# Expert weights loaded as half the rows by 512 columns, and units of work of four output tiles

## The chip, the cores and the metric

One NeuronCore of a Trainium2 chip runs the whole program. The metric is device time in microseconds (us) of one execution. Engines are named as the profile names them: PE (TensorE matmuls), PEld (TensorE weight loads), DVE (VectorE), ACT (ScalarE), POOL (GpSimd), SP (SyncE, which only issues DMAs here).

## The reference

A decoder layer on 1024 tokens of width 1024. A mixer (gated linear attention and a diagonal state-space model) comes first; the change does not touch it. The second half is a mixture of 32 experts, of which each token takes four:

```python
def expert_block(args):
    xblk, e = args
    gu = xblk @ w_gu[e] + b_gu[e]              # w_gu[e]: 1024 x 2048
    g, up = gu[:, :D_FF], gu[:, D_FF:]
    g = jnp.minimum(g, SWIGLU_LIMIT)
    up = jnp.clip(up, -SWIGLU_LIMIT, SWIGLU_LIMIT)
    act = (up + 1.0) * (g * jax.nn.sigmoid(SWIGLU_ALPHA * g))
    return act @ w_down[e] + b_down[e]         # w_down[e]: 1024 x 1024
...
out = jnp.zeros((N + 1, D_), f32).at[tok_buf].add(yb.astype(f32) * w_buf[:, None])[:N]
```

All weights are float32, 12 MB an expert. After the experts come a norm and the residual.

## The kernel before

**Sizes.** Experts are sorted by the number of their tokens; the expert of rank r has room for `CAPS[r]` tokens (396 for the first, 36 for the last). I call this number C. Eight groups of four ranks (`GROUPS`) are worked on one after the other: [204, 96, 172, 108], [184, 116, 180, 104], [272, 92, 140, 80], [164, 128, 164, 120], [396, 40, 88, 56], [260, 60, 148, 112], [248, 48, 192, 92], [252, 68, 228, 36] tokens, in this order within a group.

**Weights.** A piece of weights (`chunks`) is 1 MB: all 1024 rows by 256 columns, which lie in SBUF as [128 partitions, 8 row blocks, 256 columns]. SP loads it into one of six staging slots (`ST`, the A buffers 0 to 5). `split_chunk` (L1594 to L1597) makes two fp16 parts of it: ACT writes the high part (`wh`, L1596), then DVE the low part (`wl`, L1597), side by side in one of seven slots (`WH`, `WL`, in the buffers B0, B1, C0, C1, E0, E1, A6, used in turn). After a piece is split, SP may load the piece six further on into its staging slot.

**Products.** `products` (L1615 to L1620) makes one output tile, 128 columns of weights by C tokens: for each of eight row blocks three matmuls (high by high, high by low, low by high), 24 in all, into PSUM.

**Units.** The work on PE is a list of units. In a group's gate-up stage there are four rounds (c = 0 to 3), and in each round one unit for each of the four experts: two tiles of the gate from one piece, then two tiles of the up part from the next piece, 96 matmuls. In the down stage each expert has four units in a row, each of two tiles from one piece, 48 matmuls. Where C is over 256 a unit is halved (one tile of each kind), since two tiles don't fit one PSUM bank; both halves then use the same pieces.

**Order.** The program is written out in one loop over the units, each engine runs its own instructions in the order written. For unit i the loop writes: what is left of the unit two before (`second`: the activations as fp16 parts), the evictions of the unit before (`first`: ACT reads PSUM at L1661, L1664 or L1683; DVE clips and multiplies), the splits, and then the products of unit i. The splits go as far as this line allows (L1760), where `done` is the last piece that the units before the last one are through with and `NWS` is 7:

```python
split_to((max(done + NWS, need) if i > 2 else need) + 1)
rest = run_unit(*u)
```

In the down stage the loop also writes, behind a unit's products, the transposes and fp16 parts of the next group's tokens (`xg_split`, L1610), and for finished halves of an expert's results `put_out`/`moe_out`: PE transposes (L1697), ACT copies into one of three buffers (L159, tile A), POOL scatters with accumulation to `ff_d` in DRAM (L1699).

Of the kernel before, what the change touches and what calls it, by code (L numbers as in the profile page):

```python
# [26 lines left out]
RD = 1.0 / 32.0                            # 1 / sqrt(D)  # L27
# [4 lines left out]
LS = T + 128                              # places in an expert's list of tokens  # L32
CAPS = [396, 272, 260, 252, 248, 228, 204, 192, 184, 180, 172, 164, 164, 148, 140, 128, 120, 116, 112, 108, 104, 96,
        92, 92, 88, 80, 68, 60, 56, 48, 40, 36]
# ranks that are worked on together, with about the same number of tokens in each group
GROUPS = [[6, 21, 10, 19], [8, 17, 9, 20], [1, 23, 14, 25], [11, 15, 12, 16], [0, 30, 24, 28], [2, 27, 13, 18],
          [4, 29, 7, 22], [3, 26, 5, 31]]
WS = 4096.0                               # scales of the fp16 parts of weights and tokens
# [9 lines left out]
def hybrid_layer_kernel(ctx: ExitStack, tc: tile.TileContext, I, out):  # L48
# [7 lines left out]
    # SBUF: one tile of plain float32 regions, and slots that change their type from phase to phase  # L56
# [104 lines left out]
    # ------------------------------------------------------------------ the order of the work: a clock of the tensor  # L161
    # engine's work, and background work that is put between it when its turn has come
# [3 lines left out]
    def step(g):  # L166
        """Puts out the next part of a piece of background work; False at its end."""
# [37 lines left out]
    def finish(*which):  # L205
        """Puts out all that is left of some background work, or of all."""
# [7 lines left out]
    # ------------------------------------------------------------------ constants  # L214
    TB = 64                                   # KB: temporaries
# [6 lines left out]
    gmask = small(128)                        # [j, i] = j <= i within a 64 chunk  # L222
# [13 lines left out]
    vecs = view(TB + 1, 128)                  # 24 rows  # L236
    v2 = view(TB + 1.5, 128)                  # 48 rows
# [10 lines left out]
    walpha = small(256)                       # rows 0..15 and again 16..31, zeros below  # L248
# [3 lines left out]
    rw2 = walpha.rearrange("p (k e) -> p k e", k=8)            # in the place of what is used before  # L252
# [18 lines left out]
    # c, transposed  # L271
# [16 lines left out]
    def ada_row(i, mod_c, on_v):  # L288
        """a row of the modulation, turned into columns; the tiles on_v are summed on the vector engine first"""
# [69 lines left out]
    def s5_prep():  # L359
# [75 lines left out]
        # unit rotator of 8 steps, |a|^8  # L435
# [10 lines left out]
        # f = (a - 1) / lambda  # L446
# [27 lines left out]
        # Bbar  # L474
# [4 lines left out]
    def s5_rot():  # L479
        # the tables e^{i phi n}  # L480
# [17 lines left out]
    def s5_c():  # L498
        # C, transposed; D on the diagonal of the 16x16 blocks
# [28 lines left out]
    def s5_ca():  # L528
        # C A^d, and K[d] = Re(C A^d Bbar) replicated over s, with zeros before
# [1117 lines left out]
    def run_unit(kind, x, c, js, n):  # L1647
# [29 lines left out]
        if c % 2 == 0 and js[0] == 0:  # L1677
            yT_of[x.r] = y_place(C)
# [235 lines left out]
```

## Time and profile before

| | before |
|---|---|
| time, median of 3 runs | 2072.47 us (2068.52 to 2079.74) |
| profiled execution, first to last instruction (span) | 2069.1 us |
| median above this span | 3.4 us |
| PE busy | 1831.0 us, 88% |
| DVE, ACT, POOL busy | 71%, 63%, 23% |
| SP's DMA queue | 469.51 MB, 72.4% of 16 engines' span |

The page gives one execution, the span from its first to its last instruction. It shows nothing outside the span, so the profiled execution's own time is taken as its span. Busy PE is not PE at its peak: a waiting PE and one on half its clock can both look busy, so starts of matmuls are read beside it. The expert part runs from the first product at 603.5 us to the last at 2003.8 us.

### The profile page before, as it was taken

To read this page: it belongs to the slowest core of one execution; us is meant where nothing else is said; L and a number is where in the kernel's file an instruction comes from. 1 tells how busy PE (TensorE), PEld (TensorE's weight loads), DVE (VectorE), ACT (ScalarE), POOL (GpSimd) and SP (SyncE) were. 2 spreads that over 40 slices of the span, in tenths; PEclk is the share of its full clock that TensorE was granted. 3 is DMA by queue.
4 is the path that set the end of the run, shared out by engine and by line. 5 is a ranking of instruction groups with operands and counts; after the bars stand their busy time and mean duration, and the time that the engine had idled before them with its cause. 6 is when DMAs were issued, how large, how long until landed. Compare 5 with 4: busy or idle time off the path is not lost. (4 is left out here: it accounts for less than half of the span.)

```text
span 2069.1 us, 53438 instructions
## 1 busy us (share of the span) xinstructions
PE 1831.0 (88%) x22354; PEld 1634.6 (79%) x22354; DVE 1465.9 (71%) x2361; ACT 1294.2 (63%) x1997; POOL 473.8 (23%) x495
## 2 busy tenths in 40 slices
PE   7678899999978999998998998999699899999950
PEld 3566788787868998997987998766599789999950
DVE  5766536567748976985894897686589668878825
ACT  3524133643326877886885887776688677888831
POOL 4720112204531033024013303201320230140033
PEclk9999899999979999999999999999899999999985
DMA  9076554323379999999999999999799999999964
GB/s 310 31 206 123 157 173 147 128 83 123 112 211 307 335 336 304 348 329 291 343 346 267 322 349 327 310 325 315 221 320 349 284 286 334 338 331 342 345 177 170
DMA packets 493413, 540.83 MB, mean 261 GB/s; under 512 B 41234, under 2 KB 459248, under 8 KB 493136
## 3 DMA queue, kind: packets, MB, share of 16 engines
q1 hardware_dynamic: 456112, 469.51, 72.4%
q0 software_dynamic: 30384, 60.49, 11.7%
q10 hardware_dynamic: 6672, 7.38, 1.1%
q8 instruction: 177, 2.90, 0.6%
q14 instruction: 68, 0.56, 0.1%
HBM read 489.57 MB, written 45.61 MB: 259 GB/s over the span
## 5 line engine op out<-in xcount | busy, mean ns | idle before, releaser
L1597 DVE SCALAR_TENSOR_TENSOR E<-A,E 128x2048 f16<-128x2048 f32 x110 | 250.5, 2289 | 92.1 <-ACT E L1596 89.4
L1699 POOL DMA_INDIRECT ff_d<-A,S x102 | 205.9, 2019 | 464.4 <-ACT A L159 252.4
L1597 DVE SCALAR_TENSOR_TENSOR B<-A,B 128x2048 f16<-128x2048 f32 x110 | 250.7, 2290 | 73.8 <-ACT B L1596 73.4
L1597 DVE SCALAR_TENSOR_TENSOR C<-A,C 128x2048 f16<-128x2048 f32 x110 | 250.5, 2289 | 52.0 <-ACT C L1596 48.8
L1620 PE MATMUL mm<-S,B 128*128 128x148 f16 (+27 forms) x1328 | 260.1, 234 | 2.9 <-DVE B L1597 2.4
L1618 PE MATMUL mm<-S,B 128*128 128x148 f16 (+27 forms) x1328 | 260.0, 234 | 2.8 <-ACT B L1596 2.1
L1618 PE MATMUL mm<-S,E 128*128 128x164 f16 (+27 forms) x1344 | 253.1, 231 | 10.2 <-ACT S L1683 10.2
L1619 PE MATMUL mm<-S,B 128*128 128x148 f16 (+27 forms) x1328 | 259.8, 233 | 0.6 <-issue 0.4
L1620 PE MATMUL mm<-S,E 128*128 128x164 f16 (+27 forms) x1344 | 253.2, 230 | 1.5 <-issue 1.5
L1619 PE MATMUL mm<-S,E 128*128 128x164 f16 (+27 forms) x1344 | 253.0, 230 | 0.9 <-issue 0.9
L1618 PE MATMUL mm<-S,C 128*128 128x92 f16 (+25 forms) x1296 | 241.2, 230 | 3.8 <-ACT S L1683 3.8
L1620 PE MATMUL mm<-S,C 128*128 128x92 f16 (+25 forms) x1296 | 241.0, 229 | 0.0
L1619 PE MATMUL mm<-S,C 128*128 128x92 f16 (+25 forms) x1296 | 240.9, 229 | 0.0
L1602 POOL DMA_INDIRECT S<-hn_d,S x51 | 80.5, 1578 | 687.6 <-PE tr L1610 647.8
L1596 ACT ACTIVATE B<-A 128x2048 f16<-128x2048 f32 x110 | 209.9, 1924 | 31.7 <-DMA A<-in_exp_w_gu_dram 27.7
L1596 ACT ACTIVATE E<-A 128x2048 f16<-128x2048 f32 x110 | 210.1, 1923 | 17.7 <-DMA A<-in_exp_w_gu_dram 9.0
L1596 ACT ACTIVATE C<-A 128x2048 f16<-128x2048 f32 x110 | 209.9, 1924 | 16.9 <-DMA A<-in_exp_w_gu_dram 9.6
L1619 PEld LDWEIGHTS <-E 128*128 128x128 f16 x1760 | 167.7, 99 | 18.8 <-issue 11.3
L1619 PEld LDWEIGHTS <-C 128*128 128x128 f16 x1760 | 171.6, 100 | 11.0 <-issue 4.3
L159 ACT ACTIVATE A<-ax,S 128x512 f32<-128x512 f32 (+17 forms) x102 | 68.5, 685 | 178.1 <-DMA ff_d<-A,S 154.2
L1618 PEld LDWEIGHTS <-B 128*128 128x128 f16 x1760 | 170.7, 99 | 10.7 <-ACT B L1596 2.4
L1619 PEld LDWEIGHTS <-B 128*128 128x128 f16 x1760 | 171.3, 100 | 9.7 <-issue 3.1
(345 smaller groups left out, 5130.0 us busy)
## 6 DMA issues: line engine op xcount, KB each, us to landing
A<-in_exp_w_gu_dram SPq DMA_DIRECT2D x256, 1024.0 KB
A<-in_exp_w_down_dram SPq DMA_DIRECT2D x128, 1024.0 KB
S<-in_ada_w_dram POOLq DMA_DIRECT2D x64, 256.0 KB, 3.1
S<-in_ada_w_dram SPq DMA_DIRECT2D x16, 512.0 KB
S<-in_w_in_dram SPq DMA_DIRECT2D x8, 1024.0 KB
S<-in_x_dram SPq DMA_DIRECT2D x12, 512.0 KB
ff_d<-S POOLq DMA_DIRECT2D x18, 256.0 KB, 6.1
S<-in_w_out_dram SPq DMA_DIRECT2D x8, 512.0 KB
```

Source lines behind the costliest of these rows:

```text
L159: A.activation(o, i, AF.Copy, scale=scale)
L1596: i_ = A.activation(wh, st, AF.Copy, scale=WS)
L1597: i_ = V.scalar_tensor_tensor(wl, st, WS, wh, op0=OP.mult, op1=OP.subtract, accum_out=acc_col())
L1602: P.indirect_dma_start(out=x_[0:cb], out_offset=None, in_=hn2_d, in_offset=bass.IndirectOffsetOnAxis(ap=x.lt[0:cb, b, 0:1], axis=0))
L1618: i_ = PE.matmul(o, wh[:, k, cols], mh[:, k], start=(k == 0), stop=False)
L1619: PE.matmul(o, wh[:, k, cols], ml[:, k], start=False, stop=False)
L1620: i_ = PE.matmul(o, wl[:, k, cols], mh[:, k], start=False, stop=(k == 7))
L1699: P.indirect_dma_start(out=ff_d[h], out_offset=bass.IndirectOffsetOnAxis(ap=lt[0:cb, b, 0:1], axis=0), in_=yt[0:cb], in_offset=None, compu ...
```

## The change

A piece is still 1 MB, but half of the rows (four row blocks, `kh` = 0 or 1) by 512 columns, [128, 4, 512] in SBUF, so that a row of a load is 2 KB long and not 1 KB. An output tile now needs two pieces, one for each half of the rows. A unit takes two pieces and makes four output tiles of one kind: a gate unit ("g"), an up unit ("u") or a down unit ("d"), 96 matmuls each. A group's gate-up stage has two rounds (c = 0, 1) in which each expert has a g and then a u unit; in the down stage each expert has two d units. Where C is over 256 the unit is halved into two tiles, and the order is g, u of the first two tiles, then g, u of the others, with all four pieces held throughout. The buffers for gate and up results grow to four tiles: two for gates, one for ups (before three pairs of two tiles). The line that bounds the splits is the same with units counted anew (L1772).

```diff
-    ST = [carve(t_, 0, 8, 256) for t_ in SA[:-1]]
+    ST = [carve(t_, 0, 4, 512) for t_ in SA[:-1]]
...
-    sw_r = [(carve(t_, o, 512), carve(t_, o + 2, 512)) for t_, o in ((e2, 0), (e2, 4), (e3, 0))]
+    gs_r, u_t = [carve(e2, 0, 1024), carve(e2, 4, 1024)], carve(e3, 0, 1024)
...
-        for c in range(4):
+        for c in range(2):
             for r in g:
-                for js in ([(0, 1)] if CAPS[r] <= 256 else [(0,), (1,)]):
-                    units.append(("gu", ex[r], c, js, len(chunks)))
-                chunks += [(ex[r], "exp_w_gu", 1024 * q + 256 * c) for q in range(2)]
+                for js in J4 if CAPS[r] <= 256 else J2:
+                    units += [(kind, ex[r], c, js, len(chunks) + 2 * q) for q, kind in enumerate("gu")]
+                chunks += [(ex[r], "exp_w_gu", 1024 * q + 512 * c, kh) for q in range(2) for kh in range(2)]
...
-    def products(o, n, cols, mh, ml):
-        wh, wl = WH[n % NWS], WL[n % NWS]
-        for k in range(8):
-            i_ = PE.matmul(o, wh[:, k, cols], mh[:, k], start=(k == 0), stop=False)
-            PE.matmul(o, wh[:, k, cols], ml[:, k], start=False, stop=False)
-            i_ = PE.matmul(o, wl[:, k, cols], mh[:, k], start=False, stop=(k == 7))
+    def products(outs_, n, js, mh, ml):
+
+        for o, j in zip(outs_, js):
+            cols = slice(128 * j, 128 * j + 128)
+            for f_ in range(8):
+                wh, wl, k = WH[(n + f_ // 4) % NWS], WL[(n + f_ // 4) % NWS], f_ % 4
+                PE.matmul(o, wh[:, k, cols], mh[:, f_], start=(f_ == 0), stop=False)
+                PE.matmul(o, wh[:, k, cols], ml[:, f_], start=False, stop=False)
+                PE.matmul(o, wl[:, k, cols], mh[:, f_], start=False, stop=(f_ == 7))
...
+    def mm_places(n, C):
+        per = min(n, 512 // C)
+        banks = [mm_bank() for _ in range(-(-n // per))]
+        return [banks[i // per][:, i % per * C:i % per * C + C] for i in range(n)]
...
-        need = u[4] + (2 if u[0] == "gu" else 1) - 1
-        split_to((max(done + NWS, need) if i > 2 else need) + 1)
+        need = u[4] + 1
+        split_to((max(done + NWS, need) if i > 5 else need) + 1)
```

The places where the order matters below are in the last group, where the expert of 252 tokens is followed by the one of 68 and then by the one of 228. First ACT before, in the gate-up stage from the evictions of the unit of 252 tokens on. A and B, C, E with a number are the slots; a split writes a B, C, E or A6 slot from a staging slot A0 to A5; `E2_4723<-mm` are evictions from PSUM.

```order
L1661 ACTIVATE E2_4723<-mm_4735,E3_4724 128x252 x2
L1664 ACTIVATE E2_4723<-mm_4736,E3_4724 128x252 x2
L1596 ACTIVATE B1_4574<-A5_4730 128x2048
L1596 ACTIVATE C0_4575<-A0_4725 128x2048
L159 ACTIVATE S_63<-E2_4723 128x504
```

The same place of the changed kernel, ACT, from the evictions of the gate unit (L1673) and the up unit (L1680) of 252 tokens to those of the units of 68 tokens:

```order
L1673 ACTIVATE E2_4723<-ax_4737,E3_4724 128x252 x2
L1673 ACTIVATE E2_4723<-mm_4734,E3_4724 128x252 x2
L1599 ACTIVATE B0_4573<-A3_4728 128x2048
L1599 ACTIVATE B1_4574<-A4_4729 128x2048
L1680 ACTIVATE E3_4724<-mm_4735,E3_4724 128x252 x2
L1680 ACTIVATE E3_4724<-mm_4736,E3_4724 128x252 x2
L1599 ACTIVATE C0_4575<-A5_4730 128x2048
L1599 ACTIVATE C1_4576<-A0_4725 128x2048
L160 ACTIVATE S_63<-E2_4723 128x1008
L1673 ACTIVATE E2_4723<-ax_4737,E3_4724 128x68 x4
L1599 ACTIVATE E0_4577<-A1_4726 128x2048
L1599 ACTIVATE E1_4578<-A2_4727 128x2048
```

In both, two splits stand behind the evictions of the unit of 252 tokens. Before, the first of them (B1) is the second piece of the unit of 228 tokens, one unit ahead of the one that PE then works on; in the changed kernel it is C0, the second piece of the up unit of 68 tokens, also one unit ahead.

On PE before, the unit of 228 tokens passes from its first piece (B0) to its second (B1) when its gate tiles are done, behind 48 of its 96 matmuls:

```order
L1620 LDWEIGHTS B0_4573
L1620 MATMUL mm_4735<-S_63,B0_4573 128x228
L1618 LDWEIGHTS B1_4574
L1618 MATMUL mm_4736<-S_63,B1_4574 128x228
L1619 LDWEIGHTS B1_4574
```

In the changed kernel PE's up unit of 68 tokens passes from its first piece (B1) to its second (C0) behind 12 of its 96 matmuls, within the first tile, and both pieces are read until its last tile:

```order
L1626 LDWEIGHTS B1_4574
L1626 MATMUL mm_4734<-S_63,B1_4574 128x68
L1624 LDWEIGHTS C0_4575
L1624 MATMUL mm_4734<-S_63,C0_4575 128x68
L1625 LDWEIGHTS C0_4575
L1625 MATMUL mm_4734<-S_63,C0_4575 128x68
L1626 LDWEIGHTS C0_4575
```

DVE in the changed kernel at the same place: the clip (L145) and the product (L148) of the up unit of 252 tokens, the low parts of two pieces, the low part of the activations (L148 into S), and the low parts of the next two pieces.

```order
L145 TENSOR_SCALAR E3_4724<-E3_4724 128x1008
L148 SCALAR_TENSOR_TENSOR E2_4723<-E2_4723,E3_4724 128x1008
L1600 SCALAR_TENSOR_TENSOR C0_4575,A7_4732<-A5_4730,C0_4575 128x2048
L1600 SCALAR_TENSOR_TENSOR C1_4576,A7_4732<-A0_4725,C1_4576 128x2048
L148 SCALAR_TENSOR_TENSOR S_63<-E2_4723,S_63 128x1008
L1600 SCALAR_TENSOR_TENSOR E0_4577,A7_4732<-A1_4726,E0_4577 128x2048
```

Before, the same instructions stood there for 504 columns, once for every unit; now for 1008 columns, once for every g and u pair.

## Rows read from the trace of the kernel before

**Rows 1.** The page's head and part 1: busy us, share of the span, instructions.

```profile
span 2069.1 us, 53438 instructions
...
PE 1831.0 (88%) x22354; PEld 1634.6 (79%) x22354; DVE 1465.9 (71%) x2361; ACT 1294.2 (63%) x1997; POOL 473.8 (23%) x495
```

**Rows 2.** Windows by stage: start:end, length, busy by engine, PEclk, DMA share, GB/s.

```profile
603.50:677.60 74.10, 61.86 (x813) 58.09 (x813) 54.76 (x106) 48.04 (x62) 5.19 (x3) 0.89 1.02 302
677.60:726.10 48.50, 48.50 (x772) 48.50 (x770) 46.21 (x58) 40.94 (x57) 0.00 (x0) 1.00 1.10 349
893.00:964.80 71.80, 63.84 (x873) 62.08 (x871) 46.25 (x68) 49.94 (x76) 24.64 (x12) 0.93 1.05 307
...
1835.10:1936.60 101.50, 101.50 (x1548) 97.12 (x1546) 87.77 (x108) 83.74 (x116) 14.22 (x5) 1.00 1.09 341
1936.60:2003.80 67.20, 54.83 (x803) 51.92 (x800) 35.84 (x36) 40.81 (x59) 16.21 (x7) 0.94 0.87 271
603.50:2003.80 1400.30, 1305.43 (x19226) 1211.47 (x19226) 1059.28 (x1422) 1056.23 (x1487) 271.12 (x142) 0.97 1.04 317
```

**Rows 3.** Waits of PE from 600 to 2000 us: us in total, times, longest.

```profile
PE ax L1697 <- ACT S L1683: 29.2, 15, 4.4
PE tr L1610 <- DMA S<-hn_d,S: 16.9, 4, 6.5
...
PE ax L1620 <- issue: 3.1, 3, 1.5
...
PE mm L1620 <- issue: 2.0, 2, 1.5
```

**Rows 4.** Timeline of PE, last group: the first matmul of five units in a row.

```profile
1886.28 0.27 PE L1618 MATMUL mm<-S,C 128*128 128x252 f16 x1
...
1896.62 0.19 PE L1618 MATMUL ax<-S,E 128*128 128x68 f16 x1
...
1899.61 0.26 PE L1618 MATMUL mm<-S,A 128*128 128x228 f16 x1
...
1909.00 0.18 PE L1618 MATMUL ax<-S,B 128*128 128x36 f16 x1
...
1911.42 0.27 PE L1618 MATMUL mm<-S,C 128*128 128x252 f16 x1
```

**Rows 5.** Timeline of ACT behind the unit of 252 tokens.

```profile
1896.83 0.83 ACT L1664 ACTIVATE E<-mm,E 128x252 f32<-128x252 f32 x2 [0.42 <-PE mm L1620]
1897.55 3.84 ACT L1596 ACTIVATE B<-A 128x2048 f16<-128x2048 f32 x2
1901.30 0.61 ACT L159 ACTIVATE S<-E 128x504 f16<-128x504 f32 x1
...
1902.21 0.52 ACT L1664 ACTIVATE E<-mm,E 128x68 f32<-128x68 f32 x2
```

**Rows 6.** Timeline of DVE at the same place.

```profile
1897.79 0.23 DVE L147 SCALAR_TENSOR_TENSOR S<-E,S 128x72 f16<-128x72 f32 x1
1897.93 0.42 DVE L144 TENSOR_SCALAR E<-E 128x504 f32<-128x504 f32 x1
1898.38 0.68 DVE L147 SCALAR_TENSOR_TENSOR E<-E 128x504 f32<-128x504 f32 x1
1899.49 2.29 DVE L1597 SCALAR_TENSOR_TENSOR B<-A,B 128x2048 f16<-128x2048 f32 x1 [0.42 <-ACT B L1596]
...
1901.70 2.29 DVE L1597 SCALAR_TENSOR_TENSOR B<-A,B 128x2048 f16<-128x2048 f32 x1
```

**Rows 7.** Waits of ACT from 600 to 2000 us, the longest in total.

```profile
ACT A L159 <- DMA ff_d<-A,S: 133.0, 44, 11.8
```

**Rows 8.** Windows in which weights of 1 KB rows, 4 KB rows, 2 KB rows are loaded.

```profile
1176.00:1236.00 60.00, 60.00 (x964) 60.00 (x962) 54.02 (x71) 49.69 (x70) 0.00 (x0) 1.00 1.10 349
1980.00:1984.00 4.00, 4.00 (x44) 3.96 (x42) 0.00 (x0) 0.64 (x2) 0.00 (x0) 1.00 1.03 389
2032.00:2037.00 5.00, 0.00 (x0) 0.00 (x0) 1.23 (x1) 2.02 (x3) 2.00 (x1) 0.50 1.01 376
```

More of the change, by code (lines that the diff above doesn't have):

```diff
@@ L1577, in hybrid_layer_kernel @@
         for r in g:
-            for c in range(4):
-                for js in ([(0, 1)] if CAPS[r] <= 256 else [(0,), (1,)]):
-                    units.append(("dn", ex[r], c, js, len(chunks)))
-                chunks.append((ex[r], "exp_w_down", 256 * c))
+            for c in range(2):
+                for js in J4 if CAPS[r] <= 256 else J2:
+                    units.append(("d", ex[r], c, js, len(chunks)))
+                chunks += [(ex[r], "exp_w_down", 512 * c, kh) for kh in range(2)]
     def load_chunk(n):
@@ L1590, in load_chunk @@
         else:
-            x, name, col = chunks[n]
-            SP.dma_start(ST[n % NST], I[name][0][ds(x.e, 1), :, col:col + 256].rearrange("o (k p) c -> p (o k) c", p=128))
+            x, name, col, kh = chunks[n]
+            SP.dma_start(ST[n % NST], I[name][0][ds(x.e, 1), 512 * kh:512 * kh + 512, col:col + 512]
+                         .rearrange("o (k p) c -> p (o k) c", p=128))
     def split_chunk(n):
@@ L1643, in y_place @@
             put_out()
+        assert not any(o[0] < at + n and at < o[1] for o in y_open)
         y_at[0], y_at[1] = (at, at + n), at + n
@@ L1649, in run_unit, with first @@
         C, nj = x.C, len(js)
-        if kind == "gu":
-            pp_ = [mm_bank() for _ in range(2)]
-            for q in range(2):
-                for i, j in enumerate(js):
-                    products(pp_[q][:, i * C:i * C + C], n + q, slice(128 * j, 128 * j + 128), x.xh, x.xl)
-            gs, u_ = sw_r[n_sw[0] % len(sw_r)]
+        mh, ml = (x.ah, x.al) if kind == "d" else (x.xh, x.xl)
+        pp = mm_places(nj, C)
+        products(pp, n, js, mh, ml)
+        f0 = 4 * c + js[0]
+        if kind == "g":
+            x.gs = gs_r[n_sw[0] % len(gs_r)]
             n_sw[0] += 1
-            f0 = 2 * c + js[0]
+            gs = x.gs
             def first():
                 for i in range(nj):
-                    A.activation(gs[:, i * C:i * C + C], pp_[0][:, i * C:i * C + C], AF.Gelu_apprx_sigmoid,
-                                 bias=x.bias[f0 + i], scale=RS)
+                    A.activation(gs[:, i * C:i * C + C], pp[i], AF.Gelu_apprx_sigmoid, bias=x.bias[f0 + i], scale=RS)
+            return first, None
+        if kind == "u":
+            gs = x.gs
+            def first():
                 for i in range(nj):
-                    i_ = A.activation(u_[:, i * C:i * C + C], pp_[1][:, i * C:i * C + C], AF.Identity,
-                                 bias=x.bias[8 + f0 + i], scale=RS)
-                ts(u_[:, 0:nj * C], u_[:, 0:nj * C], 8.0, OP.min, -6.0, OP.max)
-                stt(gs[:, 0:nj * C], gs[:, 0:nj * C], G_MAX, u_[:, 0:nj * C], OP.min, OP.mult)
+                    A.activation(u_t[:, i * C:i * C + C], pp[i], AF.Identity, bias=x.bias[8 + f0 + i], scale=RS)
+                ts(u_t[:, 0:nj * C], u_t[:, 0:nj * C], 8.0, OP.min, -6.0, OP.max)
+                stt(gs[:, 0:nj * C], gs[:, 0:nj * C], G_MAX, u_t[:, 0:nj * C], OP.min, OP.mult)
             def second():
@@ L1673, in run_unit @@
             return first, second
-        pd = mm_bank()
-        for i, j in enumerate(js):
-            products(pd[:, i * C:i * C + C], n, slice(128 * j, 128 * j + 128), x.ah, x.al)
-        if c % 2 == 0 and js[0] == 0:
+        if js[0] == 0:
             yT_of[x.r] = y_place(C)
-        yT = yT_of[x.r]
+            y_open.append(y_at[0])
+        yT, at = yT_of[x.r], y_at[0]
         def first():
             for i, j in enumerate(js):
-                i_ = A.activation(yT[:, 2 * (c % 2) + j], pd[:, i * C:i * C + C], AF.Identity,
-                             bias=x.bias[16 + 2 * c + j], scale=RS)
-        if c % 2 == 0 or js[-1] == 0:
-            return first, None
-        at = y_at[0]
-        return first, lambda: outs.append((x, c // 2, yT, at, pe_t[0]))
+                A.activation(yT[:, j], pp[i], AF.Identity, bias=x.bias[16 + f0 + i], scale=RS)
+            if js[-1] == 3:
+                y_open.remove(at)
+                outs.append((x, c, yT, at, pe_t[0]))
+        return first, None
     n_yt = [0]
@@ L1743, in hybrid_layer_kernel @@
     for i, u in enumerate(units):
[L1744 removed]
+        if u[0] == "g" and listed < len(GROUPS) and GROUPS[listed - 1][0] == u[1].r and u[2] == 0 and u[3][0] == 0:
             for r in GROUPS[listed]:
@@ L1776, in hybrid_layer_kernel @@
                     n_todo += 1
-        pe_t[0] += (2 if u[0] == "gu" else 1) * len(u[3]) * 24 * (u[1].C / 2400 + 0.003)
+        pe_t[0] += len(u[3]) * 24 * (u[1].C / 2400 + 0.003)
         if outs and pe_t[0] - outs[0][4] > 2.0:
             put_out()
-        if todo and i + 1 < len(units) and units[i + 1][0] == "gu":
+        if todo and i + 1 < len(units) and units[i + 1][0] == "g":
             while n_todo < len(todo):
```

25 lines of the change are left out of this document (13 added, 12 removed).

## The prediction

> **What bounds the kernel now.** I read the page's head first, then windows by stage, waits, timelines. The page [rows 1] gives a span of 2069.1 us; the median of the runs is 3.4 us above it, and I add this at the end. PE's 88% is an average, so I cut the expert part by stages [rows 2]. The reader should see two kinds of stage there. A gate-up stage past the start (677.6 to 726.1, 1835.1 to 1936.6) has PE busy in its whole length at PEclk 1.00. In a down stage (893.0 to 964.8, 1936.6 to 2003.8) PE is idle for 8 to 12 us and the clock is 0.93. That gate-up stages run at PE's own pace is shown by the starts of units [rows 4]: 96 matmuls of 252 tokens take 10.34 us, of 68 tokens 2.99, of 228 tokens 9.39, of 36 tokens 2.42. That is 107.7, 31.1, 97.8 and 25.2 ns a matmul, near 0.42 ns a token plus 3 ns, and not under 25 ns; no hole lies between units. So PE is the bound there, but with little room beside it: in the last gate-up stage DVE is busy for 87.8 of 101.5 us, ACT for 83.7, and the DMA share is 1.09 [rows 2]. What PE loses now it loses in the down stages and at the start, mostly waiting for ACT's evictions and for gathered tokens [rows 3]. ACT itself stands 133.0 us, in 44 waits, for scatters to land before it may refill a result buffer [rows 7]; only part of this reaches PE.
>
> **What does not change.** Matmuls, columns, weight loads, bytes, splits, evictions, gathers and scatters keep their numbers and sizes. DVE's clips, products and low parts of activations become half as many and twice as long, which saves less than 0.1 us each on an engine that is not the bound. None of it shortens PE's own work, so in a gate-up stage there is nothing to win.
>
> **The loads.** With 1 KB rows the stream moves 349 GB/s at a full DMA; the result loads in 2 KB rows moved 376, the residual in 4 KB rows 389 [rows 8]. A piece (1.049 MB) thus takes 3.00 us now and 2.79 then, 7% less. In gate-up stages PE does not wait for loads, so this is hidden. At the start it is not: the eight units from 603.5 to 677.6 take 74.1 us, the next eight with the same tokens 48.5 [rows 2]. Some 22 pieces (16 used, six ahead) times 0.21 us give 5 us back. Bounds: 15 us back, if the larger first units also cover the gathers; 5 us lost, if PE stands longer for the second piece, which it now needs 12 matmuls into its first tile. I take -5. The Trainium skill, "DMA: Bandwidth & Descriptors", section Specifications, says that transfers from 512 B on run at line rate. By that rule 1 KB and 2 KB rows are alike and this term is 0. Rows 8 speak for a small gain, in short windows.
>
> **The pieces come too late for small experts.** This is the large term. In both kernels the splits written at a unit reach three pieces past it, and they stand behind the evictions of the unit before, so they begin when that unit ends. Before, the first of these pieces is wanted in the middle of the next unit; now after 12 of its 96 matmuls. And behind a small expert's gate unit now comes its up unit, just as short, where before the next expert came.
>
> I work one visit out, 252, 68, 228 tokens; time 0 is the end of the up unit of 252. ACT: the last evictions run to 0.93, as now (1896.62 to 1897.55), then two splits to 2.85 and 4.77 [rows 5]. DVE: the clip starts at 1.31, as now (1897.93) [rows 6]. Its 504 columns take 0.42 us; twice as many at most 0.84, I take 0.7. The product takes 0.68 for 504 columns and 0.23 for 72 (the low part of activations, same instruction), so 1.04 ns a column and 1.2 for 1008. DVE is free at 3.2, and the low parts of two pieces, 2.2 us apart [rows 6], are there at 5.5 and 7.7. PE: the gate unit of 68 runs from 0 to 2.99 on pieces split before. The up unit does 12 matmuls, wants the second piece at 3.4 and gets its low part at 5.5: **2.1 us lost**. It ends at 8.1. DVE then has the low part of 1008 activations (1.2) and the next piece: 11.2. The gate unit of 228 starts at 8.1 and wants that piece 1.2 later, at 9.3: **1.9 us lost**. During the 9 us units of 228 ACT and DVE catch up. The same steps give 4.8 for 36 tokens (2.7 and 2.1), so 8.8 a round, and with two rounds 17.6 us for the last group, which now loses nothing in this stage.
>
> For the other groups, with unit lengths from tokens: 48 and 92 behind 248 and 192 cost 5.4 and 1.6, 14 us in two rounds. 60 behind 260: 4.4, so 8.8. 92 and 80: 1.9 and 2.4, so 8.5. In the group of 396, 40, 88, 56 three small experts stand in a row and DVE never catches up: 11.9 a round, 23.8; the kernel before already loses the short waits of 3.1 and 2.0 us there, as L1620 "issue" [rows 3], so 18.8 more. The three groups of 96 to 204 tokens: 3, 1.6 and 0. Sum 72 us. Bounds: 35, if half is hidden because evictions come tile by tile and ACT runs ahead; 105, if the new waits bring the clock of these stages from 1.00 to 0.95 (between them and the down stages' 0.93 [rows 2]): 5 us in each of seven stages.
>
> **The down stages.** Here a unit took one piece and five were split ahead; now it takes two, with three ahead. Eleven experts have under 100 tokens. By the steps above, without DVE's clip and product, their second piece is late by 1.8 us for 68 tokens, of which PE's transposes in between hide about half: 1 us each, 11 us. What ACT waits for scatters falls now on its splits with less in hand: if most of the 133.0 us [rows 7] that do not show at PE (29.2 do [rows 3]) came through, up to 70. Against it, a DMA with 7% more room may land scatters and gathers sooner; at best the 29.2 and 16.9 us at PE [rows 3] shrink by two thirds, 30. I take +11, with bounds of -30 and +70, near the lower end because splits only fall behind where the experts are small.
>
> **Sum.** 2069.1 - 5 + 72 + 11 = 2147; with 3.4 us, **2150 us**, 4% slower.
>
> **Rivals.** *Faster: the DMA was the hidden bound of the down stages.* Place: scatters and gathers in the down stages and the loads of the start. If with less DMA work their landings come early enough, PE's waits there go (29.2 and 16.9 us), the clock of eight stages of about 70 us goes from 0.93 to 1.00 (up to 39 us), and the start gives 15: 100 us. It decides from the point where this is over the 72 us of late pieces: 2072 - 100 + 72 = 2044. For it speak ACT's 133.0 us; against it that in the same stages the loads are not what PE waits for. Chance 0.18. *No change:* gains of the down stages and losses of the gate-up stages cancel, or ACT and DVE run ahead and only few visits lose: 2072, 0.11. *Much slower:* the lower clock (33 us more) and ACT's scatter waits (60 more) come on top: 2240, 0.13. The forecast holds 0.58; its own range is 2105 to 2200. For it speaks that the order of splits and evictions is fixed in the program, against it that durations of one visit stand for all.
>
> **How the numbers follow.** The likeliest case gives 2150. From 2055 to 2215 lie that case, no change, a part of the faster case and a third of the much slower one; beyond are 0.12 below and 0.08 above. A measurement of this kernel can tell 0.5% (10 us) from no change: faster 0.18, same 0.11, slower 0.71.
>
> **What would show it.** In the timeline of the last gate-up stage the up unit of 68 tokens should take about 5 us and not 3, with a wait behind its 12th matmul that DVE's low part ends; the window of that stage should be near 119 us (101.5 now), with DVE's share of it lower. The gate-up stages of 164, 128, 164, 120 and 184, 116, 180, 104 should keep their length. PE's waits should name splits (L1599, L1600) with some 60 us or more, where now evictions lead. The DMA share in gate-up stages should fall from 1.09 to about 0.9. The forecast is wrong if units of small experts keep their length, or if the down stages together change by more than the gate-up stages.

## The result and the profile after

The changed kernel takes 2139.11 us (median of 4 runs, 2126.77 to 2146.1), the kernel before 2073.38 us beside it (2068.52 to 2079.74): ratio 1.031, 95% interval 1.027 to 1.035. It is 3.1% slower, 66 us.

Page of the changed kernel, head and part 1:

```profile
span 2137.6 us, 53186 instructions
...
PE 1843.7 (86%) x22354; PEld 1638.8 (77%) x22354; DVE 1440.9 (67%) x2151; ACT 1291.0 (60%) x1927; POOL 465.3 (22%) x495
```

Against [rows 1] the span is 68.5 us longer, with the same matmuls; DVE and ACT do the same work in fewer instructions. Windows by stage (start:end, length, busy by engine, PEclk, DMA share, GB/s): the first gate-up stage, a down stage, a gate-up stage of middle-sized experts, the last two stages, the whole expert part.

```profile
605.20:725.20 120.00, 107.78 (x1581) 103.22 (x1580) 98.05 (x140) 87.69 (x111) 5.07 (x3) 0.96 0.96 321
...
894.60:962.90 68.30, 62.17 (x874) 60.23 (x871) 42.67 (x63) 48.37 (x73) 21.16 (x13) 0.98 0.95 293
...
1149.30:1247.90 98.60, 96.84 (x1542) 96.61 (x1541) 86.93 (x86) 84.56 (x107) 13.65 (x7) 1.00 1.03 366
...
1886.70:2001.50 114.80, 104.35 (x1542) 97.90 (x1540) 82.69 (x83) 79.68 (x104) 11.01 (x4) 0.97 0.86 291
2001.50:2078.30 76.80, 57.52 (x807) 53.57 (x804) 36.33 (x38) 40.13 (x56) 16.06 (x8) 0.90 0.74 232
605.20:2078.30 1473.10, 1319.94 (x19229) 1216.62 (x19228) 1033.94 (x1212) 1052.40 (x1415) 263.44 (x143) 0.96 0.90 301
```

The first gate-up stage was 122.6 us [rows 2: 74.1 + 48.5] and is 120.0. The last was 101.5 with PE never idle and is 114.8, with 10 us of PE idle and a lower DMA share (0.86 after 1.09): everybody waits a little, nobody is full. The last down stage grew from 67.2 to 76.8.

Waits of PE from 600 to 2080 us of the changed kernel (us in total, times, longest):

```profile
PE mm L1626 <- DVE E L1600: 22.8, 16, 2.1
PE mm L1626 <- DVE B L1600: 22.6, 17, 2.1
PE ax L1709 <- ACT S L1696: 20.9, 8, 5.8
PE mm L1626 <- DVE C L1600: 19.6, 15, 2.1
PE tr L1613 <- DMA S<-hn_d,S: 18.0, 2, 11.9
PE mm L1624 <- ACT E L1599: 11.6, 3, 10.7
...
PE tr L1613 <- DVE S L148: 2.6, 4, 1.4
```

In [rows 3] evictions and gathers led, and no split stood among the longest. Now the low parts of pieces (L1600) lead, with up to 2.1 us at a time; all rows with L1600, these and five shorter ones, make 92.7 us. Of these, 56.2 us in 47 waits lie in the gate-up stages, where the kernel before stood 2.4 us in two waits for low parts.

One place of it, the up unit of 68 tokens behind the units of 252 (compare [rows 4]). PE:

```profile
1907.83 0.19 PE L1624 MATMUL ax<-S,E 128*128 128x68 f16 x1
...
1910.82 0.19 PE L1624 MATMUL mm<-S,A 128*128 128x68 f16 x1
...
1911.22 0.19 PE L1625 MATMUL mm<-S,B 128*128 128x68 f16 x1
...
1913.10 0.20 PE L1626 MATMUL mm<-S,B 128*128 128x68 f16 x1 [1.68 <-DVE B L1600]
...
1915.68 0.26 PE L1624 MATMUL mm<-S,B 128*128 128x228 f16 x1
...
1918.64 0.27 PE L1626 MATMUL mm<-S,C 128*128 128x228 f16 x1 [1.43 <-DVE C L1600]
```

The gate unit takes 2.99 us, the up unit 4.86: 12 matmuls on its first piece (A, the slot A6), two with the high part of its second (B, the slot B0), and then it stands 1.68 us for that piece's low part. The gate unit of 228 tokens stands 1.43 us in the same way. ACT and DVE at the same time:

```profile
1908.03 0.83 ACT L1680 ACTIVATE E<-mm,E 128x252 f32<-128x252 f32 x2 [3.92 <-PE mm L1626]
1908.75 3.71 ACT L1599 ACTIVATE B<-A 128x2048 f16<-128x2048 f32 x2
```

```profile
1908.90 0.69 DVE L145 TENSOR_SCALAR E<-E 128x1008 f32<-128x1008 f32 x1 [2.75 <-ACT E L1680]
1909.62 1.21 DVE L148 SCALAR_TENSOR_TENSOR E<-E,E 128x1008 f32<-128x1008 f32 x1
1910.74 2.29 DVE L1600 SCALAR_TENSOR_TENSOR B<-A,B 128x2048 f16<-128x2048 f32 x1
```

ACT was idle for 3.92 us and DVE for 2.75 before they could evict and clip; only then come the splits. The low part ends at 1912.95, 5.12 us after the up unit of 252 ended, and PE goes on.

### The profile page after: what moved, and what is told of

Read it like the earlier page. It is cut to its first block, busy times and chain, and to the rows that moved or that the text cites. A ratio compares the mean times of both kernels' runs of the same rounds, so it can differ in the third digit from the quotient of the medians.

```text
span 2137.6 us, 53186 instructions
## 1 busy us (share of the span) xinstructions
PE 1843.7 (86%) x22354; PEld 1638.8 (77%) x22354; DVE 1440.9 (67%) x2151; ACT 1291.0 (60%) x1927; POOL 465.3 (22%) x495
## 5 line engine op out<-in xcount | busy, mean ns | idle before, releaser
L1600 DVE SCALAR_TENSOR_TENSOR E<-A,E 128x2048 f16<-128x2048 f32 x110 | 249.7, 2288 | 105.0 <-ACT E L1599 105.0
L1600 DVE SCALAR_TENSOR_TENSOR B<-A,B 128x2048 f16<-128x2048 f32 x110 | 249.8, 2289 | 82.3 <-ACT B L1599 82.2
L1600 DVE SCALAR_TENSOR_TENSOR C<-A,C 128x2048 f16<-128x2048 f32 x110 | 249.8, 2289 | 77.7 <-ACT C L1599 77.5
L1626 PE MATMUL mm<-S,E 128*128 128x92 f16 (+29 forms) x1320 | 253.3, 231 | 23.3 <-DVE E L1600 22.8
L1626 PE MATMUL mm<-S,B 128*128 128x92 f16 (+29 forms) x1312 | 246.9, 230 | 22.6 <-DVE B L1600 22.6
L1624 PE MATMUL mm<-S,E 128*128 128x92 f16 (+29 forms) x1320 | 254.6, 231 | 11.9 <-ACT E L1599 11.6
L1626 PE MATMUL mm<-S,C 128*128 128x92 f16 (+28 forms) x1260 | 237.7, 229 | 20.5 <-DVE C L1600 19.6
L1625 PE MATMUL mm<-S,E 128*128 128x92 f16 (+29 forms) x1320 | 253.9, 230 | 0.4 <-issue 0.4
L1624 PE MATMUL mm<-S,B 128*128 128x92 f16 (+29 forms) x1312 | 248.4, 231 | 4.7 <-ACT B L1599 4.7
L1625 PE MATMUL mm<-S,B 128*128 128x92 f16 (+29 forms) x1312 | 247.9, 230 | 0.2 <-DVE S L148 0.2
L1624 PE MATMUL mm<-S,C 128*128 128x92 f16 (+28 forms) x1260 | 238.6, 230 | 0.8 <-ACT C L1599 0.6
L1625 PE MATMUL mm<-S,C 128*128 128x92 f16 (+28 forms) x1260 | 238.3, 229 | 0.0
L1605 POOL DMA_INDIRECT S<-hn_d,S x51 | 67.6, 1326 | 774.5 <-PE tr L1613 493.7
L1626 PEld LDWEIGHTS <-E 128*128 128x128 f16 x1760 | 171.3, 100 | 43.8 <-DVE E L1600 36.0
L1624 PEld LDWEIGHTS <-E 128*128 128x128 f16 x1760 | 172.0, 100 | 19.7 <-ACT E L1599 13.2
```

What stands on the lines that cost most here:

```text
L1600: i_ = V.scalar_tensor_tensor(wl, st, WS, wh, op0=OP.mult, op1=OP.subtract, accum_out=acc_col())
L1605: P.indirect_dma_start(out=x_[0:cb], out_offset=None, in_=hn2_d, in_offset=bass.IndirectOffsetOnAxis(ap=x.lt[0:cb, b, 0:1], axis=0))
L1624: PE.matmul(o, wh[:, k, cols], mh[:, f_], start=(f_ == 0), stop=False)
L1625: PE.matmul(o, wh[:, k, cols], ml[:, f_], start=False, stop=False)
L1626: PE.matmul(o, wl[:, k, cols], mh[:, f_], start=False, stop=(f_ == 7))
```

## Experiments

**Theory:** the second piece of a unit is wanted too soon after its split is written (late pieces). **Rivals:** the 2 KB rows or the load stream cost the time; the coarser units do (evictions for four tiles, activations all at once, ACT's waits for scatters). All kernels but one are variants of the changed one. Each ratio is against runs of the kernel before on the same chip. A stage runs from its first product to the next stage's first product; gate-up and down are sums over eight stages of the one profiled execution, which lies up to 5 us from the median, in experiment 4 11 us above it.

| kernel | median us | ratio (95%) | gate-up | down |
|---|---|---|---|---|
| before | 2073 to 2076 | 1 | 826.0 | 574.3 |
| changed | 2139.1 | 1.031 (1.027 to 1.035) | 878.9 | 594.3 |
| 1 rows outer | 2092.8 | 1.009 (1.006 to 1.013) | 853.0 | 577.8 |
| 2 splits first | 2151.9 | 1.039 (1.035 to 1.043) | 884.1 | 608.1 |
| 3 rows of 1 KB | 2150.6 | 1.036 (1.032 to 1.040) | 896.5 | 592.0 |
| 4 old pieces | 2115.7 | 1.019 (1.016 to 1.022) | 866.9 | 591.3 |
| 5 reach 8 | 2093.3 | 1.009 (1.007 to 1.010) | 855.1 | 568.4 |
| 6 rows outer, reach 8 | 2089.9 | 1.006 (1.004 to 1.008) | 850.2 | 574.4 |
| 7 before, reach 8 | 2089.1 | 1.007 (1.004 to 1.009) | 831.1 | 586.5 |
| 8 rows outer, splits first | 2090.0 | 1.006 (1.004 to 1.008) | 836.6 | 592.0 |
| 9 in turn | 2126.3 | 1.024 (1.021 to 1.028) | 877.7 | 587.6 |
| 10 rows outer, in turn | 2089.0 | 1.007 (1.005 to 1.009) | 848.6 | 581.6 |
| 11 all three | 2091.1 | 1.008 (1.006 to 1.010) | 846.1 | 576.8 |
| 12 rows outer, in turn, reach 8 | 2081.0 | 1.002 (1.000 to 1.004) | 837.8 | 570.0 |

**1. Rows outer.** The loop over the halves of the rows stands outside that over the tiles:

```diff
-        for o, j in zip(outs_, js):
-            cols = slice(128 * j, 128 * j + 128)
-            for f_ in range(8):
-                wh, wl, k = WH[(n + f_ // 4) % NWS], WL[(n + f_ // 4) % NWS], f_ % 4
...
+        for kh in range(2):
+            wh, wl = WH[(n + kh) % NWS], WL[(n + kh) % NWS]
+            for i, (o, j) in enumerate(zip(outs_, js)):
+                cols = slice(128 * j, 128 * j + 128)
+                for k in range(4):
+                    f_ = 4 * kh + k
...
```

> The changed kernel, but a unit makes the first half of the rows of all its tiles and then the second half, so that its second piece is wanted after 48 of 96 matmuls and not after 12. Late pieces (my theory): the second piece of the up unit of 68 tokens came 1.9 us late, and is now wanted 1.1 us later, that of a unit of 36 tokens 2.8 late and wanted 0.9 later, that of large units is no longer waited for. The gate-up stages, 879 us, should fall to 840 to 855, the whole to about 2105 us (2090 to 2120). Long rows or the load stream as the cause: 2139, no change. Coarser units (evictions for four tiles, activations at once) or ACT's waits for scatters as the cause: 2139 as well.

(Tiles that share a PSUM bank are then one accumulation, which the first of them starts.) Measured 2092.8, at the low end of what late pieces say. Pieces, buffers, units, splits and evictions are those of the changed kernel; only the place of want moved, and 46 of the 66 us went. That speaks against both rivals for this part. Its waits of PE:

```profile
PE ax L1712 <- ACT S L1699: 40.6, 14, 9.8
...
PE mm L1629 <- DVE E L1600: 10.5, 11, 2.1
PE mm L1629 <- DVE C L1600: 9.6, 13, 1.4
PE mm L1629 <- DVE B L1600: 8.1, 11, 2.1
PE mm L1629 <- DVE A L1600: 8.0, 8, 2.1
```

With three shorter rows the waits for low parts are 42 us, less than half. The wait of result transposes for evictions (L1699 here, L1696 in the changed kernel) grew from 20.9 to 40.6: part of what was gained comes back there. Gate-up is 853.0, near the upper end of what was expected, and the down stages gave 16.5 us, which no theory had named.

**2. Splits first.**

```diff
+        need = u[4] + 1
+        if i > 5:
+            split_to(max(done + NWS, need) + 1)
         if rest:
             rest[0]()
...
-        need = u[4] + 1
-        split_to((max(done + NWS, need) if i > 5 else need) + 1)
+        split_to(need + 1)
```

> The changed kernel, but the splits of a unit are written ahead of the evictions of the unit before, for the same pieces. Late pieces behind evictions (my theory): ACT and DVE use the idle time in which they now wait for the last product of a unit, the waits on L1599 and L1600 (110 us at PE) go for the most part, the gate-up stages fall from 879 to 830 to 845, the whole to about 2090 us (2075 to 2105). Against it: evictions begin up to 4 us later, and if PSUM banks or activations are then waited for, the time stays at 2130 to 2150. Long rows or the load stream as the cause: 2139.

Measured 2151.9: the theory's number missed by 60 us. ACT's waits in it:

```profile
ACT S L160 <- DVE E L148: 157.8, 61, 5.1
```

The up unit of 68 tokens now had its pieces 3.7 us before it wanted them, as meant. But DVE's clip and product stand behind two low parts, so ACT waits for that product with its copy of the activations (157.8 us, 16.6 in the changed kernel), the next splits stand behind the copy, and large gate units wait in place of small up units; PE's result transposes wait 53.5 us for evictions. An engine that works in order passes a wait on. Where the splits stand relative to the evictions is a cause of late pieces, but moving them alone trades one wait for another.

**3. Rows of 1 KB.**

```diff
-            SP.dma_start(ST[n % NST], I[name][0][ds(x.e, 1), 512 * kh:512 * kh + 512, col:col + 512]
-                         .rearrange("o (k p) c -> p (o k) c", p=128))
+            for h in range(2):
+                SP.dma_start(ST[n % NST][:, :, 256 * h:256 * h + 256],
+                             I[name][0][ds(x.e, 1), 512 * kh:512 * kh + 512, col + 256 * h:col + 256 * h + 256]
+                             .rearrange("o (k p) c -> p (o k) c", p=128))
```

> The changed kernel, but every piece is loaded by two DMAs of 256 columns each, so that rows of a load are 1 KB as before; all else stays. Late pieces (my theory): within 10 us of 2139, the DMA share of the gate-up stages back near 1.0 and over, the start of the experts up to 5 us longer. Long rows as a cause of the loss: clearly under 2139, towards 2072. Long rows as a gain that hides a larger loss: above 2150.

2150.6, just past the edge between two of the answers. The interval overlaps that of the changed kernel, so the whole alone settles little. The first gate-up stage, where ACT's splits wait for loads (15.2 us here, 6.2 in the changed kernel), says more (120.0 in the changed kernel):

```profile
601.80:732.50 130.70, 110.46 (x1581) 106.05 (x1580) 98.15 (x140) 87.91 (x111) 4.68 (x3) 0.92 0.99 305
```

In this stage long rows gain 10.7 us. They are no cause of the loss. The edit also makes two DMAs of each piece; that the rows and not the number of DMAs count here is borne out by experiment 4, which has rows of 1 KB in one DMA a piece (see the last section).

**4. Old pieces** (all rows by 256 columns) with the new units:

```diff
-    ST = [carve(t_, 0, 4, 512) for t_ in SA[:-1]]
+    ST = [carve(t_, 0, 8, 256) for t_ in SA[:-1]]
...
-            SP.dma_start(ST[n % NST], I[name][0][ds(x.e, 1), 512 * kh:512 * kh + 512, col:col + 512]
+            SP.dma_start(ST[n % NST], I[name][0][ds(x.e, 1), :, col + 256 * kh:col + 256 * kh + 256]
...
-            cols = slice(128 * j, 128 * j + 128)
+            cols = slice(128 * (j % 2), 128 * (j % 2) + 128)
+            wh, wl = WH[(n + j // 2) % NWS], WL[(n + j // 2) % NWS]
...
-                wh, wl, k = WH[(n + f_ // 4) % NWS], WL[(n + f_ // 4) % NWS], f_ % 4
+                k = f_
```

> The changed kernel with its units of four tiles of one kind, but pieces as before, all rows by 256 columns: the first piece of a unit serves its first two tiles, the second is wanted after 48 of 96 matmuls. Late pieces (my theory): as with the rows in the outer loop, about 2105 us (2090 to 2120), within 10 us of that run; a loss stays because the up unit follows at once behind a small gate unit. Long rows as the cause: 2072. Coarser units as the cause: 2139.

2115.7 is inside the range of late pieces, but 23 us above experiment 1 and not within 10. So the coarser units by themselves cost 39 us (1.019). Late pieces are the largest new wait here too: PE's waits for low parts add to 46 us. That this is since a small up unit now stands at once behind a small gate unit is argued from the order of the program, no run takes it apart. Against experiment 1, with the second piece wanted at the same matmul, pieces with rows of 2 KB are worth 20 us by the ratios (1.019 to 1.009). The two profiled executions are 31 us apart; of these 9 lie in the first stage (126.7 and 117.3), 13 in the down stages. So the change can be walked in three steps: units +39, shape of the pieces -20, earlier want +46, together 65 us. Experiment 3 puts rows alone at 10 us (1.031 to 1.036), so the second step is known to within 10 us only.

**5. Reach 8.** One staging slot becomes a slot for a split piece:

```diff
-    ST = [carve(t_, 0, 4, 512) for t_ in SA[:-1]]
-    WT.append(SA[-1])
+    ST = [carve(t_, 0, 4, 512) for t_ in SA[:-2]]
+    WT += SA[-2:]
```

> The changed kernel with one staging slot turned into a slot for split pieces: eight split, five staged, where it was seven and six. The same line then reaches one piece further, so both pieces of a unit are written for splitting two units ahead; the second piece of the up unit of 68 tokens stands behind the evictions of the gate unit of 252 tokens, 10 us earlier. Late pieces (my theory): that unit takes 3 us again and not 4.8, the gate-up stages fall from 879 to 835 to 850, the down stages from 594 to about 580, the whole to about 2085 us (2070 to 2100). Load stream as the cause: 2139 or more, since one load less can be under way. Coarser units as the cause: 2139.

2093.3 as the theory said, with another remedy than in experiment 1: nothing moved within a unit, the splits are only written one piece earlier. In the last group the up unit of 68 tokens takes 3.83 us in the first round, 0.67 of them a wait for no engine, and 2.99 in the second; PE's waits for low parts fell from 92.7 to 28 us. Two different remedies give the same 46 us. The expectation of 835 to 850 for gate-up was missed by 5, that of 580 for the down stages by 12 the other way; on the waits for no engine see the last section.

**6. Both.** The edits of 1 and 5.

> Rows in the outer loop and eight split pieces together. Late pieces (my theory): nearly nothing is left to wait for in the gate-up stages but the group of 396, 40, 88, 56 tokens, gate-up 830 to 840, the whole 2065 to 2082 us, equal to the kernel before within what can be told. If something else in the coarser units costs the 17 us that the rows in the outer loop left: 2085 to 2095.

2089.9: the second answer. The remedies don't add; some 13 us are left (1.006). In the profiled execution they lie in the gate-up stages (850.2 against 826.0, down 574.4 against 574.3). PE stands there 16 us for low parts (2.4 before) and 10 us for no engine (6 before), so a part of the rest is late pieces again.

**7. The kernel before, with the edit of 5** as control.

> The kernel before with eight split pieces and five staged, as a control. Late pieces (my theory): its gate-up stages do not wait for pieces, so there is nothing to gain, within 10 us of 2073. If a deeper reach helps any kernel, by its down stages or its group of 396 tokens: 2050 to 2062. If five staging slots starve the loads: above 2083.

2089.1, slower (1.004 to 1.009): the third answer, and the 10 us of the theory are missed. The loads have one slot less, and ACT's splits in it wait for them:

```profile
ACT E L1596 <- DMA A<-in_exp_w_gu_dram: 24.7, 15, 7.0
ACT A L1596 <- DMA A<-in_exp_w_gu_dram: 21.5, 18, 2.5
```

All such waits add to 95 us, 54 in the kernel before. So reach 8 is bought with up to 13 us where it isn't needed, and a deeper reach does not help by itself: its gain in the changed kernel goes with late pieces. The price lies mostly in the down stages here (12 us, 5 in gate-up), where experiment 6 lost nothing, so it hardly accounts for what is left there; no run takes the two apart.

**8. Rows outer, and splits first, then activations, then evictions.** Experiment 2's edit, with the loop over `late` behind the splits as well.

> Rows in the outer loop, and per unit the order splits, activations of the unit two before, evictions of the unit before (where splits ahead of evictions cost time, ACT waited 158 us on its copy of activations for DVE's product, which stood behind two low parts). Order as the cause of that loss: ACT's wait on that copy falls under 60 us, pieces come early, the whole 2070 to 2085 us. Late evictions as the cause (result transposes then wait for ACT's evictions, 53 us there): 2093 to 2110.

2090.0. ACT's wait on its copy fell to 14.2 us and gate-up to 836.6, as order predicts, but the down stages took 592.0, since result transposes wait 56.8 us for late evictions, as the other answer said. Both answers were half right, and the total is no better.

**9. In turn.** Gates of two experts, then the up parts of both, so that no 192 matmuls of a small expert stand in a row:

```diff
-            for r in g:
-                for js in J4 if CAPS[r] <= 256 else J2:
-                    units += [(kind, ex[r], c, js, len(chunks) + 2 * q) for q, kind in enumerate("gu")]
-                chunks += [(ex[r], "exp_w_gu", 1024 * q + 512 * c, kh) for q in range(2) for kh in range(2)]
+            if gi + c == 0:
+                pairs = [[r] for r in g]
+            elif CAPS[g[0]] > 256:
+                pairs = [g[:1], g[1:3], g[3:]]
+            else:
+                pairs = [g[:2], g[2:]]
+            for pr in pairs:
+                for q, kind in enumerate("gu"):
+                    if CAPS[pr[0]] <= 256:
+                        for k_, r in enumerate(pr):
+                            units.append((kind, ex[r], c, J4[0], len(chunks) + 2 * (len(pr) * q + k_)))
...
+                chunks += [(ex[r], "exp_w_gu", 1024 * q + 512 * c, kh) for q in range(2) for r in pr for kh in range(2)]
```

> The changed kernel with another order of units: in a round the gates of two experts and then the up parts of the same two (of 252, 68, 252, 68 tokens), but for the very first round and for experts of over 256 tokens. So 96 and not 192 matmuls of a small expert stand in a row, and the up unit of 68 tokens follows one of 252. Late pieces (my theory): by the same steps the up unit of 252 still loses about 1 us and the gate unit of 228 about 1.3, where 1.9 and 1.5 were lost at 68 and 228 tokens and 2.8 and 1.5 at 36 and 252; gate-up 850 to 860, the down stages as they were (594), the whole about 2112 us (2098 to 2122). If what is left beside late pieces is PE's own issue of 192 short matmuls in a row: the waits on issue vanish from the up units as well, the whole nearer 2098. Neither: 2139.

2126.3: 13 us gained, half of what was expected and outside all the ranges; its interval just touches that of the changed kernel. The gain isn't where it was looked for: gate-up is 877.7 after 878.9 (850 to 860 were expected), the down stages, which the edit leaves alone, are 6.7 us shorter. Late pieces are still at 87 us in PE's waits (92.7 before the edit); in the gate-up stages most moved from the small up units to the units behind small ones.

**10. Rows outer, in turn.** Edits of 1 and 9.

> Rows in the outer loop and gates and up parts of two experts in turn. With rows in the outer loop alone 2093 us; with three other remedies for late pieces beside or in place of it 2090 to 2093, each with PE waits on issue in the up units of 36, 48, 56 and 68 tokens, 1.1 to 2.7 us each. If these are the rest (192 short matmuls in a row): they go, the up unit of 36 tokens takes 2.4 us, gate-up falls from 853 to about 832, the whole to about 2072 us (2064 to 2082). If the rest is late pieces or evictions for four tiles: 2085 to 2095.

2089.0: the second answer. The waits on issue went from the gate-up stages (2.1 us in experiment 1, 0.2 here). With 33 us of waits for low parts left (42 in experiment 1), the order in turn gives nothing that can be told.

**11. All three.** Edits of 1 and 9, and the order of 8 in the gate-up stages alone.

> Rows in the outer loop, gates and up parts in turn, and in the gate-up stages alone splits ahead of activations and evictions (over all stages this order gave the shortest gate-up, 837 us, but 592 in the down stages against 578, since evictions there came late). If both causes are right: gate-up 820 to 828, down 575 to 585, the whole about 2068 us (2058 to 2078), equal to or under the kernel before. If late evictions cost as much here: 2080 to 2092.

2091.1: the second answer, the theory is missed. PE's waits for low parts shrank against experiment 10, that of its result transposes for evictions grew (37.8 to 48.6 us), which is what late evictions say, and one for a PSUM place that ACT had not emptied came (4.3 us).

**12. Rows outer, in turn, reach 8.** Edits of 1, 5 and 9.

> Rows in the outer loop, gates and up parts of two experts in turn, and eight split pieces. With the first and the third alone PE still waits in the gate-up stages 20 us for low parts and 12 us on issue, the whole 2090 us. If what is left adds up (late pieces and short matmuls in a row): the issue waits go, gate-up falls from 850 to 838 to 845, down stages 570 to 578, the whole 2072 to 2082 us, near the kernel before but not under it, since that kernel's gate-up is 826. If every remedy only uncovers the next wait, as with rows in the outer loop and either order: 2085 to 2095.

2081.0, the first answer; ratio 1.002 (1.000 to 1.004), so within 0.5% of the kernel before, and no better. Against experiment 6 the order in turn is worth 9 us, and PE's waits on issue are what fell; those for low parts are 21 us in both. Experiment 6, then experiment 12:

```profile
PE mm L1629 <- issue: 8.3, 7, 2.5
PE mm L1627 <- issue: 2.4, 3, 1.2
```

```profile
PE mm L1640 <- issue: 1.4, 2, 0.9
PE mm L1638 <- issue: 1.4, 2, 0.8
```

Its last gate-up stage is as long as before the change, and PE full:

```profile
1847.10:1948.20 101.10, 101.10 (x1540) 96.67 (x1540) 84.98 (x86) 82.90 (x105) 12.90 (x5) 1.00 0.98 346
```

## Why the prediction was right, step by step

The forecast of 2150 us was 11 us above the measured 2139, in its range and with its sign; late pieces are shown as the main cause by experiments 1 and 5, which take 46 of the 66 us away by two different remedies. That the total came so near is partly luck, since the terms missed in both directions. Its terms came out differently:

**Start, -5.** The first product comes 1.7 us later and the first gate-up stage is 2.6 shorter: -0.9. The step mis-sized both halves: long rows give about 10 us there (experiments 3 and 4). The coarser units take 4.1 back (126.7 in experiment 4 against 122.6 before) and the early want of the second piece 2.7 (120.0 against 117.3 in experiment 1), each from one profiled execution.

**One visit.** Worked out from the end of the up unit of 252: ACT's splits at 0.93, DVE free at 3.2, low part at 5.5, 2.1 us lost, the up unit about 5 us long. Measured: 0.92, 2.91, 5.12, 1.68 and 4.86. The unit of 228 lost 1.43 and not 1.9, the up unit of 36 tokens stood 2.12 us and not 2.7. That clips and products of double length save less than 0.1 us each was too low: 0.15 each (0.69 and 1.21 against twice 0.42 and 0.68 [rows 6]).

**Gate-up, +72.** The seven stages past the first grew by 55.5 us (703.4 to 758.9): 13.3 in the last group (17.6 forecast), 10.5 with 48 and 92 (14), 15.4 with 396, 40, 88, 56 (18.8), 5.0 with 60 (8.8), 10.1 with 272, 92, 140, 80 (8.5), 1.3 in the two of middle-sized experts, which were to keep their length (4.6 was booked for them and the first stage together). Every visit of the last group was priced 0.4 to 0.6 us too high: 0.24 of it since the clip starts 1.07 and not 1.31 us after the unit's end, the rest since the work of DVE behind it was a little shorter; there are 47 waits in all. In the group of 272 the sum was nearly right for another reason: the first two units of 272 tokens stood 0.95 and 1.93 us for their pieces, and behind that the clock was lower for a while (0.73 from 975 to 980 us), while the units of 92 and 80 lost under 1 us each.

**Clock, in the bound of 105.** It fell, but for short stretches:

```profile
1886.70:1940.20 53.50, 49.31 (x692) 46.59 (x689) 36.47 (x37) 35.97 (x46) 11.01 (x4) 1.00 0.92 307
1940.20:1947.00 6.80, 5.75 (x98) 4.67 (x99) 6.80 (x8) 6.80 (x13) 0.00 (x0) 0.50 0.70 226
1947.00:2001.50 54.50, 49.28 (x754) 46.65 (x753) 39.42 (x40) 36.91 (x47) 0.00 (x0) 1.00 0.81 284
```

Of the six waits of PE in this stage one (2.12 us, at 36 tokens) was followed by the lower of the two levels (0.50, 1.2 of 2.4 GHz); the unit of 252 behind it took 12.0 and not 10.3 us, so 1.6 us. What the prediction booked as the piece after 36 tokens (2.1) was this; for that piece itself PE did not wait.

**Down, +11.** 20.0 us (574.3 to 594.3), inside the bounds, but nearly twice the forecast, and made up otherwise: the step "PE's transposes hide about half, 1 us each" failed. Down units stand up to 2.1 us for a low part, also those of large experts (2.0 us at 228 and at 180 tokens). In the eight down stages PE's waits for splits went from none to 54 us, 37 of them for low parts. Against it its waits for evictions shrank from 42 to 21 us, those for tokens from 20 to 13. The longest wait only changed its name. The last down stage, PE before, PE after, and ACT before and after:

```profile
PE mm L1618 <- ACT S L1683: 10.2, 1, 10.2
```

```profile
PE mm L1624 <- ACT E L1599: 10.7, 1, 10.7
PE mm L1626 <- DVE E L1600: 4.2, 2, 2.1
PE ax L1626 <- DVE B L1600: 2.0, 1, 2.0
```

```profile
ACT A L159 <- DMA ff_d<-A,S: 21.4, 3, 10.8
...
ACT A L160 <- DMA ff_d<-A,S: 21.5, 3, 11.3
```

In both kernels PE waits 10 us for what stands on ACT behind its wait for a scatter (10.2 and 11.3 us at that place): once an eviction, now a split. The 4.2 and 2.0 us behind it are new.

**The end.** The time behind the last product fell from 65.3 to 59.3 us, which no step held. It is 59 to 60 in every run with the new units and six staging slots, 65 to 66 with five; why stays open. Sum: -0.9 + 55.5 + 20.0 - 6.0 = 68.6, the spans differ by 68.5.

**Rivals.** The DMA share of the expert part fell from 1.04 [rows 2] to 0.90, yet ACT still waits 123.8 us in 44 waits for scatters (133.0 in 44 [rows 7]): fewer, longer packets hardly made them land earlier, so the faster case had no ground. The much slower case needed a clock of 0.95 in all gate-up stages; only the one with three small experts in a row had it (0.95, the others 0.96 to 1.00).

## What to carry to other kernels

Two buffers that are consumed together need the second one almost as early as the first: count the matmuls from a unit's start to the first use of each piece, and set this against where its preparation stands in the program behind evictions. Moving the first use (a loop order) or the preparation (one buffer more) repaired the same 46 us, while moving the preparation ahead of the evictions handed the wait to another engine that works in order. When two remedies for one wait don't add, look for the next wait behind it, and for what of the first one both have left: here short matmuls in a row (9 us) and 16 us of late pieces in the gate-up stages.

## What the runs showed of the hardware

**Stalls in long rows of short matmuls.** In every run in which the pieces were in time, up units of 36, 48 and 68 tokens in most visits stood 0.7 to 2.5 us for no engine (experiments 2, 5, 6, 8). The kernel before has three such stalls of 1.3 to 1.5 us, in its units of 56 tokens behind those of 40 and 88 ("issue" in [rows 3]). Experiment 5, PE in the up unit of 36 tokens, and the DMA queues from 1901.5 to 1905 us (packets, MB, share):

```profile
1904.51 0.21 PE L1626 MATMUL mm<-S,A 128*128 128x36 f16 x1 [2.26 <-issue]
```

```profile
q8 instruction: 1, 0.02, 2.0%
```

A single packet of the instruction queue (2.90 MB in 177 packets in the changed kernel, so 16 KB each) lies in this stretch, and one at the other visit of the same unit (2.23 us). Both stalls come 170 matmuls after the start of the small gate unit (4.25 us at 25.2 ns each), as they do at 36 tokens in experiments 2, 6 and 8. A third packet ends 0.6 us ahead of the stall of 0.67 us at 68 tokens; eight others lie in the same gate-up stage of experiment 5 without such a stall. That PE waited for these instructions to arrive is inferred from the place, not shown; shown is that the stalls go when 96 and not 192 short matmuls stand in a row (experiment 12). In the changed kernel's last gate-up stage they don't show; PE stands in those units for a late piece. The Trainium skill, "Runtime: NRT & Kernel Launch", section Instruction fetch mechanics, says that instructions are refilled in blocks of 16 KiB, and that the cost of crossing a block is mostly hidden. The size agrees with the trace; that it is hidden does not hold here, if the inference is right.

**Rows of 2 KB against 1 KB.** With PE never idle and the DMA share over 1, the changed kernel moves 379 GB/s:

```profile
1160.00:1240.00 80.00, 80.00 (x1271) 80.00 (x1269) 71.81 (x74) 68.38 (x87) 7.89 (x5) 1.00 1.05 379
```

Before it was 349 at a share of 1.10 [rows 8], 8% less, near the 7% that the prediction took. The Trainium skill, "DMA: Bandwidth & Descriptors", section Specifications, has line rate from 512 B on, by which rows of 1 KB and 2 KB are alike and the start gains nothing. The measurement decides against it: with rows of 1 KB the first gate-up stage takes 10.7 us more (experiment 3). One stretch of the second gate-up stage in the changed kernel, in experiment 3 (rows of 1 KB, two DMAs a piece) and in experiment 4 (rows of 1 KB, one DMA a piece):

```profile
820.00:880.00 60.00, 59.79 (x921) 59.53 (x919) 53.65 (x55) 49.43 (x65) 0.00 (x0) 1.00 1.04 374
...
820.00:880.00 60.00, 59.46 (x949) 59.19 (x947) 54.21 (x56) 50.41 (x66) 2.17 (x1) 1.00 1.09 349
...
820.00:880.00 60.00, 59.69 (x959) 59.33 (x956) 53.83 (x56) 49.61 (x63) 4.54 (x4) 1.00 1.09 348
```

The rate goes with the length of the rows, not with the number of DMAs.
